# A half pass of the attention scores in two row groups of TensorE: 2.5 passes instead of 3, and 1.5 instead of 2

## The chip, the cores and the metric

One core of one Trainium2 chip. The time is the device time of one execution in microseconds. Three runs of the kernel before gave 3068.02 us (median), 3061.11 and 3082.16.

## The reference, cut to what matters

One layer of a hybrid diffusion transformer on 2048 latent and 256 context tokens, all of it in float32. Two kinds of attention read the same modulated input; the queries are the 2048 latent tokens, the keys all 2304.

```python
q_mla = jnp.concatenate([q_nope, q_rope], axis=-1)     # 8 heads, 64 + 32 features
k_mla = jnp.concatenate([k_nope, broadcast(k_r)], axis=-1)   # the 32 rotary features are shared by the heads
s = jnp.einsum('bhqd,bhkd->bhqk', q, k) * scale        # the scores; softmax over all keys; then p @ v
...
s1 = jnp.einsum('bhqd,bhkd->bhqk', q1, k1) * scale     # 4 heads, two maps of 64 features each
s2 = jnp.einsum('bhqd,bhkd->bhqk', q2, k2) * scale
p = softmax(s1) - lam * softmax(s2)                    # then p @ v
```

After that come gates, an output projection for each kind, a merge, a last projection and a layer norm.

## The kernel before

**Precision.** Float32 operands are split into a high part, rounded to the array's 32-bit form, and a low part, the rest. A product is the sum of high x high, high x low and low x high. Queries and keys are stored in scratch memory with both parts (`qn_s`, `qr_s`, `kn_s`, `kr_s` for the first kind, `dq_s`, `dk_s` for the second; the last index but one is the feature, an axis of 2 the part).

**Stages.** First the projections (0 to 930 us in the profile): weights are loaded, split and multiplied with the transposed inputs in blocks of 512 tokens; `up` and `tiles_qk` write queries and keys to scratch through `rdma`, on SyncE's queue. Then the attention (930 to about 2640 us), then the gated output projections and the last one.

**The attention.** A unit is 256 queries of one head. The units of the two kinds take turns, two of the first (`mla_soft`) and one of the second (`diff_soft`), 64 and 32 in all; the values' products of a unit (`mla_av` at L723 and L728, `diff_av` at L710) run four units later, in pieces between the pieces of the scores, and the projections of the remaining gates (`gate_units`, tiles `pf`) fill in. The order on each engine is set when the program is made, by priorities and a model of the machine. `softmax_tile` makes the scores of 128 queries against all 2304 keys, in three groups of 768 keys. A group has a PSUM tile of two banks (1024 places, 768 used: 512 in the first bank, 256 in the second), of which there are three in turn; the products are at L669. VectorE reads the group at L670 with one instruction that scales and keeps the running extreme; ScalarE takes the exponential of all 2304 (L683). `transposed` makes two 16-bit parts (ScalarE L693, GpSimd L694) and has DMA transposes on SyncE's queue (L695) write them to the `pt` tiles that the values' products read.

**The passes.** The first kind has 96 features, in 96 of the array's 128 rows, and three passes: high x high, high x low, low x high, so 3 x 2 products a group. The second kind keeps the two parts of its keys one above the other, 64 + 64 rows, and its queries twice: one pass with the queries' high part gives high x high and high x low, a second with the queries' low part gives low x high and low x low, so 2 x 2 products. Each product loads its weights, 128 queries, anew. The narrow value products at L728 use 64 of the array's columns, two key tiles at a time in the two halves of the columns.

**Loads.** `load_k` and `load_q` fetch keys once a head and queries once a unit through `ldma` (L604), on ScalarE's queue from the fourth unit on. For the first kind that is two loads a group of keys and two a unit of queries; for the second kind one load a group of keys and two a unit of queries.

Of the kernel before, what the change touches and what calls it, by code (L numbers as in the profile page):

```python
# [61 lines left out]
def layer_kernel(ctx: ExitStack, tc: tile.TileContext, x, c, ctxt, c_ctx, w_mod, b_mod, w_in,  # L62
# [21 lines left out]
    kn_s = [dram(f"kn{t}", [P, 2, NT], F32) for t in range(4)]  # L84
    kr_s = dram("kr", [32, 2, NT], F32)
# [30 lines left out]
    def rsqrt(tp, ms, n):  # L116
        """1/sqrt(ms) of [P, n], one Newton step after the table's root"""
# [10 lines left out]
    def row_rsqrt(tp, ps, s2, cnt, eps):  # L128
        """1/sqrt(sum of squares over the partitions / cnt + eps), on all partitions: [P, 256]"""
# [24 lines left out]
    # the sums of the exponentials: by token, of the heads of both kinds  # L154
# [4 lines left out]
    with ExitStack() as st:  # L159
# [41 lines left out]
        # lamc: -lam, 1 + NT |lam|, shift of the first map  # L201
# [4 lines left out]
        # the log of about 2^15 / (1 + NT |lam|), from the bits of the float  # L206
# [69 lines left out]
        def weights(c0, m):  # L276
# [3 lines left out]
            for j0 in range(0, KT, nj):  # L280
# [3 lines left out]
                # the narrow tile's parts lie side by side, for one pass  # L284
# [20 lines left out]
        def project(w, bi, m, sub):  # L305
            """one tile's product with a block, features by tokens; of a wide tile, 256 tokens by features"""
# [29 lines left out]
        def paired(tiles, blocks):  # L336
            """the tiles (column, width, what to do with a block's product) in pairs, block by block"""
# [24 lines left out]
        def tiles_qk(blocks):  # L362
# [4 lines left out]
            def done(t):  # L367
                m = P if t >= 0 else 32

                def f(bi, pp, n, k0, i0):  # L370
# [14 lines left out]
                    if t < 0:  # L385
                        rdma(kr_s[:, :, k0:k0 + n], s[:m, :, :n])
                        return
# [83 lines left out]
        def up(ui, cn):  # L471
# [12 lines left out]
            for tt in range(2):  # L484
                pb = two(wkv, 2, cn[0], tt * 256)
                s = sq.tile([P, 2, 2, 256], F32R, tag="st", name="kst")
                split(pb, s[:, 0], s[:, 1])
                for a in range(2):
                    rdma(kn_s[2 * tt + a][:, :, k0:k0 + 256], s[:, :, a, :])
# [76 lines left out]
        # for the gates that are left for the attention's idle cycles  # L566
# [11 lines left out]
    with ExitStack() as st:  # L578
# [21 lines left out]
        # the first loads must not hold up the scalar engine, which still works on the projections  # L600
# [60 lines left out]
        def softmax_tile(qk, ks, scale, shift, zsum):  # L661
            s = spool.tile([P, NT], F32, tag="s", name="s")
            z = sm.tile([P, 4], F32, tag="z", name="z")
            for g in range(3):
                ps = ps_s.tile([P, 1024], F32, tag="ps", name="ps")
                for i, (qa, sel) in enumerate(qk):
                    ka = sel(ks[g])
                    for c0, n in ((0, 512), (512, 256)):
                        pe.matmul(ps[:, c0:c0 + n], qa, ka[:, c0:c0 + n], start=(i == 0), stop=(i == len(qk) - 1))  # L669
                dve.tensor_scalar(s[:, g * 768:(g + 1) * 768], ps[:, :768], -scale, 3e38 if g == 0 else z[:, g - 1:g],  # L670
                                  op0=ALU.mult, op1=ALU.min, accum_out=z[:, g:g + 1])
            # the exponent's shift must not push the largest one over: it vanishes, or falls, as |max| grows
# [43 lines left out]
        def mla_av(pts, vv, dst):  # L716
            """both parts of the values by the probabilities' high part; the values' high part by the low part,
            two key tiles at once in halves of the array's columns"""
# [18 lines left out]
        def load_q(kind, h, u):  # L737
            q0 = u * 256
            if kind == 0:
                qt = qp_[0].tile([P, 2, 256], F32R, tag="q0", name="q0")  # L740
                ldma(qt[0:64], qn_s[h // 2][(h % 2) * 64:(h % 2) * 64 + 64, :, q0:q0 + 256])
                ldma(qt[64:96], qr_s[h // 4][(h % 4) * 32:(h % 4) * 32 + 32, :, q0:q0 + 256])
# [6 lines left out]
        def mla_soft(h, u, qt, ks, pts):  # L749
            for i in range(2):  # L750
                qs = qt[0:96, :, i * P:(i + 1) * P]
                k_hi, k_lo = (lambda k: k[0:96, 0, :]), (lambda k: k[0:96, 1, :])
# [308 lines left out]
```

## Time and profile before

| what | us |
|---|---|
| median of 3 runs | 3068.02 (3061.11 to 3082.16) |
| the profiled execution, its span from first to last instruction | 3066.9 |
| projections, 0 to 930 | 930 |
| attention, 930 to 2640 | 1710 |
| output, 2640 to 3067 | 427 |

The page gives no other time for the profiled execution than its span. Busy times of engines overlap each other; a busy time of TensorE (PE) counts each product until its modelled end, so that products which follow closely overlap, and the distance from start to start is what one costs. PEld is the loading of the weights, which runs under the product before it.

### The profile page before, as it was taken

What the parts mean: (1) busy time and instruction counts of PE and PEld (TensorE: products, weight loads), DVE (VectorE), ACT (ScalarE), POOL (GpSimd) and SP (SyncE); (2) the same over time, 40 slices, a digit from 0 to 9 for tenths busy, and PEclk for the clock granted to TensorE, in tenths of its full rate; (3) what the DMA queues carried; (4) which work ended last, traced back from release to release, by engine and by line L of the source; (5) the groups of instructions that cost most, each with busy time, mean ns of one, the idle gap of its engine ahead of it and who ended that gap; (6) DMA issues with size and microseconds to landing.
All of it is one profiled execution on the core that took longest, in us unless ns stands there. A gap on an engine that the chain in (4) does not pass through costs nothing. (4 is left out here: it accounts for less than half of the span.)

```text
span 3066.9 us, 44697 instructions
## 1 busy us (share of the span) xinstructions
PE 2754.2 (90%) x16177; PEld 2233.1 (73%) x16177; DVE 1972.1 (64%) x3583; ACT 1446.4 (47%) x1757; POOL 1558.5 (51%) x922
## 2 busy tenths in 40 slices
PE   7999999999998988978987889989788987888998
PEld 5888888879776766756665676767566765888986
DVE  4476300024857877859887688787687889675454
ACT  3333222233325656647666567666566666321110
POOL 2442222232534756646665567576466655464344
PEclk9999999999999989989999999999899988999999
DMA  8567533264587999999999999999999999976542
GB/s 252 134 181 226 155 92 98 89 222 141 150 256 171 198 178 204 198 187 211 194 206 202 218 219 216 194 216 189 189 213 201 201 207 178 257 208 198 185 139 85
DMA packets 1273377, 571.93 MB, mean 186 GB/s; under 512 B 950250, under 2 KB 1222336, under 8 KB 1273156
## 3 DMA queue, kind: packets, MB, share of 16 engines
q1 hardware_dynamic: 1149448, 463.59, 70.2%
q10 hardware_dynamic: 123708, 105.49, 15.0%
q8 instruction: 127, 2.08, 0.3%
q14 instruction: 94, 0.77, 0.1%
HBM read 224.16 MB, written 118.30 MB: 112 GB/s over the span
## 5 line engine op out<-in xcount | busy, mean ns | idle before, releaser
L694 POOL TENSOR_TENSOR hl<-s,hl 128x1152 f16<-128x1152 f32 x378 | 937.7, 2497 | 542.1 <-ACT hl L693 479.7
L669 PE MATMUL ps<-k,q 96*128 96x256 f32 (+3 forms) x3840 | 858.0, 364 | 110.0 <-DVE s L670 101.5
L669 PEld LDWEIGHTS ps<-k,q 96*128 96x128 f32 (+1 forms) x3840 | 632.3, 200 | 243.8 <-DVE s L670 134.9
L683 ACT ACTIVATE s<-s,z 128x2304 f32<-128x2304 f32 x256 | 567.1, 2216 | 145.7 <-DVE z L681 65.6
L693 ACT CAST hl<-s 128x1152 f16<-128x1152 f32 x384 | 432.3, 1147 | 397.9 <-DMA pt<-hl 226.6
L670 DVE TENSOR_SCALAR_CACHE_REDUCE s<-ps,z 128x768 f32<-128x768 f32 x512 | 517.7, 1013 | 156.6 <-PE ps L669 142.1
L112 PE MATMUL pp<-hT,w 128*128 128x512 f32 (+1 forms) x896 | 349.2, 392 | 5.5 <-DVE qa L331 2.8
L113 PE MATMUL pp<-hT,w 128*128 128x512 f32 (+1 forms) x896 | 350.9, 392 | 0.2 <-DVE hT L266 0.2
L114 PE MATMUL pp<-hT,w 128*128 128x512 f32 (+1 forms) x896 | 349.7, 391 | 0.0
L108 POOL TENSOR_TENSOR w<-raw,w 128x512 fp32r<-128x512 f32 (+1 forms) x126 | 163.5, 1303 | 358.5 <-ACT w L105 343.7
L670 DVE TENSOR_SCALAR_CACHE_REDUCE s<-ps 128x768 f32<-128x768 f32 x256 | 243.4, 951 | 51.4 <-PE ps L669 40.3
L710 PE MATMUL po<-pt,vd 128*128 128x256 f16 x1728 | 241.4, 284 | 31.4 <-DMA pt<-hl 31.1
L723 PE MATMUL po<-pt,va 128*128 128x256 f16 x1152 | 175.5, 294 | 68.3 <-DMA pt<-hl 62.8
L710 PEld LDWEIGHTS <-vd 128*128 128x128 f16 x1728 | 158.6, 102 | 91.3 <-issue 55.6
L112 PEld LDWEIGHTS pp<-hT,w 128*128 128x128 f32 x896 | 169.8, 190 | 44.7 <-DVE qa L331 3.2
L773 DVE SCALAR_TENSOR_TENSOR s<-s,w 128x2304 f32<-128x2304 f32 x64 | 199.3, 3114 | 0.5
L113 PEld LDWEIGHTS pp<-hT,w 128*128 128x128 f32 x896 | 169.7, 189 | 38.5 <-POOL hT L266 0.9
L114 PEld LDWEIGHTS pp<-hT,w 128*128 128x128 f32 x896 | 169.9, 190 | 37.9
L723 PEld LDWEIGHTS <-va 128*128 128x128 f16 x1152 | 106.4, 104 | 120.4 <-issue 79.3
L995 PE MATMUL pz<-wz,yt 128*128 128x512 f32 x768 | 179.6, 396 | 0.8 <-DVE z L998 0.8
L108 POOL TENSOR_TENSOR fw<-fraw,fw 128x512 fp32r<-128x512 f32 x84 | 124.2, 1479 | 90.9 <-ACT fw L105 79.9
L995 PEld LDWEIGHTS pz<-wz,yt 128*128 128x128 f32 x768 | 144.3, 188 | 35.8 <-DVE z L998 1.3
(222 smaller groups left out, 4511.5 us busy)
## 6 DMA issues: line engine op xcount, KB each, us to landing
raw<-in_w_in_dram SPq DMA_DIRECT2D x122, 256.0 KB, 3.1
fraw<-in_w_in_dram ACTq DMA_DIRECT2D x79, 256.0 KB, 4.6
xt<-in_x_dram SPq DMA_DIRECT2D x32, 512.0 KB, 4.7
mg<-gt SPq DMA_DIRECT2D x64, 256.0 KB, 4.2
q<-dq ACTq DMA_DIRECT2D x60, 256.0 KB, 5.6
gt<-o SPq DMA_DIRECT2D x54, 256.0 KB, 2.0
gt<-fo ACTq DMA_DIRECT2D x42, 256.0 KB, 4.8
kn<-kst SPq DMA_DIRECT2D x36, 256.0 KB, 3.3
```

The costliest lines, as they stand in the source:

```text
L108: eng_lo.tensor_tensor(lo, t32, hi.bitcast(F32) if hi.dtype == F32R else hi, op=ALU.subtract)
L112: pe.matmul(ps, wh, mh, start=first, stop=False)
L113: pe.matmul(ps, wh, ml, start=False, stop=False)
L114: pe.matmul(ps, wl, mh, start=False, stop=last)
L669: pe.matmul(ps[:, c0:c0 + n], qa, ka[:, c0:c0 + n], start=(i == 0), stop=(i == len(qk) - 1))
L670: dve.tensor_scalar(s[:, g * 768:(g + 1) * 768], ps[:, :768], -scale, 3e38 if g == 0 else z[:, g - 1:g], op0=ALU.mult, op1=ALU.min, accum_ ...
L683: mark[0] = act.activation(s, s, AF.Exp, bias=b, scale=-1.0, accum_out=zsum).ins
L693: act.copy(hl[:, 0], se)
L694: (dve if shared and e else pool).tensor_tensor(hl[:, 1], se, hl[:, 0], op=ALU.subtract)
L710: pe.matmul(po, vv[:, w, kt, :], pt_part(pts, kt, l), start=(kt == 0 and i == 0), stop=(kt == NKT - 1 and i == 2))
L723: pe.matmul(po, vv[:, kt, :], pt_part(pts, kt, 0), start=(kt == 0), stop=(kt == NKT - 1))
L995: pe.matmul(pz[:, n, :], y[:, yy, k, :], wz[k][ww][:, n * 512:(n + 1) * 512], start=(k == 0 and i == 0), stop=(k == KT - 1 and i == 2))
```

## The change

The third pass of the first kind (and the second of the second kind) is cut into what is needed and packed. For the first kind, whole pass 0 has 128 rows: the query's high part of the 64 plain features against the keys' high and low parts of them. Whole pass 1 has again 128 rows: the plain low part against the keys' high part (64 rows), and twice the 32 rotary features' high part of the query, against the high and the low part of the rotary keys. The rest is 32 rows: the rotary low part against the rotary keys' high part. For the second kind the first pass stays, and the second takes the queries' low part against the keys' high part alone, 64 rows. This rest is run for the two PSUM banks in different rows of the array: bank 0 in rows 64 to 95 and bank 1 in rows 96 to 127 for the first kind, rows 0 to 63 and 64 to 127 for the second. For that the second bank's keys lie with their parts swapped, so that the part that is wanted lies in those rows. Every group now has 384 keys in each bank, and six or four products of 384 columns as before in number. VectorE reads the two 384s by a two-level pattern. `kn_s` is kept by head and part, `kr_s` by part. The loads grow: four of queries a unit of the first kind, five a group of its keys, three a group of the second kind's keys; the store of the plain keys is cut in two. Doc strings and comments that the change drops are left out here.

```diff
-    kn_s = [dram(f"kn{t}", [P, 2, NT], F32) for t in range(4)]
-    kr_s = dram("kr", [32, 2, NT], F32)
+    kn_s = [dram(f"kn{h}", [2, 64, NT], F32) for h in range(H)]
+    kr_s = dram("kr", [2, 32, NT], F32)
...
-                        rdma(kr_s[:, :, k0:k0 + n], s[:m, :, :n])
+                        rdma(kr_s[:, :, k0:k0 + n].rearrange("l d n -> d l n"), s[:m, :, :n])
...
                 for a in range(2):
-                    rdma(kn_s[2 * tt + a][:, :, k0:k0 + 256], s[:, :, a, :])
+                    for e in range(2):
+                        rdma(kn_s[4 * tt + 2 * a + e][:, :, k0:k0 + 256].rearrange("l d n -> d l n"),
+                             s[e * 64:(e + 1) * 64, :, a, :])
...
-                for i, (qa, sel) in enumerate(qk):
-                    ka = sel(ks[g])
-                    for c0, n in ((0, 512), (512, 256)):
-                        pe.matmul(ps[:, c0:c0 + n], qa, ka[:, c0:c0 + n], start=(i == 0), stop=(i == len(qk) - 1))
-                dve.tensor_scalar(s[:, g * 768:(g + 1) * 768], ps[:, :768], -scale, 3e38 if g == 0 else z[:, g - 1:g],
+                for i, part in enumerate(qk):
+                    for b in range(2):
+                        qa, ka = part(ks[g], g, b)
+                        pe.matmul(ps[:, b * 512:b * 512 + 384], qa, ka, start=(i == 0), stop=(i == len(qk) - 1))
+                dve.tensor_scalar(s[:, g * 768:(g + 1) * 768].rearrange("p (b n) -> p b n", b=2),
+                                  ps.rearrange("p (b n) -> p b n", b=2)[:, :, :384], -scale, 3e38 if g == 0 else z[:, g - 1:g],
                                   op0=ALU.mult, op1=ALU.min, accum_out=z[:, g:g + 1])
...
-                qt = qp_[0].tile([P, 2, 256], F32R, tag="q0", name="q0")
-                ldma(qt[0:64], qn_s[h // 2][(h % 2) * 64:(h % 2) * 64 + 64, :, q0:q0 + 256])
-                ldma(qt[64:96], qr_s[h // 4][(h % 4) * 32:(h % 4) * 32 + 32, :, q0:q0 + 256])
+                qt = qp_[0].tile([P, 3, 256], F32R, tag="q0", name="q0")
+                qn = qn_s[h // 2][(h % 2) * 64:(h % 2) * 64 + 64, :, q0:q0 + 256]
+                qr = qr_s[h // 4][(h % 4) * 32:(h % 4) * 32 + 32, :, q0:q0 + 256]
+                ldma(qt[0:64, 0:2], qn)
+                ldma(qt[64:128, 0], qn[:, 0])
+                ldma(qt[64:96, 1:3], qr)
+                ldma(qt[96:128, 1:3], qr)
...
+                qs = qt[:, :, i * P:(i + 1) * P]
+
+                def whole(l):
+                    return lambda k, g, b: (qs[:, l], k[:, l, b * 384:(b + 1) * 384])
+
+                def rest(k, g, b):
+
+                    r = slice(64 + b * 32, 96 + b * 32)
+                    return qs[r, 2], k[r, 1, b * 384:(b + 1) * 384]
+
+                s = softmax_tile([whole(0), whole(1), rest], ks, MLA_SCALE, LN_PSC,
...
+                    def high(k, g, b):
+                        return qs[:, 0, :], k[:, m, b * 384:(b + 1) * 384]
+
+                    def low(k, g, b):
+
+                        r = slice(b * 64, (b + 1) * 64)
+                        return qs[r, 1, :], k[r, m, b * 384:(b + 1) * 384]
+
+                    return softmax_tile([high, low], ks, DIFF_SCALE, shift, zsum)
...
-                    ldma(k[0:64], kn_s[h // 2][(h % 2) * 64:(h % 2) * 64 + 64, :, cs])
-                    ldma(k[64:96], kr_s[:, :, cs])
+                    ldma(k[:, 0, :], kn_s[h][:, :, cs].rearrange("l d n -> (l d) n"))
+                    ldma(k[0:64, 1, :], kn_s[h][0, :, cs])
+                    ldma(k[64:128, 1, 0:384], kr_s[:, :, g * 768:g * 768 + 384].rearrange("l d n -> (l d) n"))
+                    for l in range(2):
+                        ldma(k[96 - l * 32:128 - l * 32, 1, 384:768], kr_s[l, :, g * 768 + 384:(g + 1) * 768])
                 else:
-                    ldma(k, dk_s[h][:, :, :, cs].rearrange("l d m n -> (l d) m n"))
+                    cs = slice(g * 768, g * 768 + 384)
+                    ldma(k[:, :, 0:384], dk_s[h][:, :, :, cs].rearrange("l d m n -> (l d) m n"))
+                    cs = slice(g * 768 + 384, (g + 1) * 768)
+                    for l in range(2):
+                        ldma(k[(1 - l) * 64:(2 - l) * 64, :, 384:768], dk_s[h][l, :, :, cs])
```

## Rows read from the trace of the kernel before

**Rows 1.** The page's first part: busy us of each engine, share of the span, instructions.
```profile
PE 2754.2 (90%) x16177; PEld 2233.1 (73%) x16177; DVE 1972.1 (64%) x3583; ACT 1446.4 (47%) x1757; POOL 1558.5 (51%) x922
```

**Rows 2.** Busy time by stretch: us, each engine's busy us, clock, DMA share, GB/s.
```profile
core 0: us, PE busy (x) PEld busy (x) DVE busy (x) ACT busy (x) POOL busy (x), PEclk, DMA share, GB/s
0.00:930.00 930.00, 884.66 (x4738) 735.63 (x4739) 365.89 (x676) 275.43 (x523) 294.94 (x254) 0.99 0.56 168
930.00:2640.00 1710.00, 1481.99 (x8996) 1151.65 (x8996) 1371.35 (x2402) 1099.83 (x1094) 1069.36 (x476) 0.92 1.09 199
```

**Rows 3.** Chain of waits, 1836 to 2640 us: shares of the stretch by line.
```profile
by line: DMA pt<-hl 19.3%; issue 14.8%; PE ps L669 11.0%; DVE s L670 10.5%; POOL hl L694 6.4%; ACT s L683 4.0%; ACT hl L693 3.4%; PE po L710 3.2%; DVE s L773 2.7%; PE po L723 2.4%; DMA fraw<-in_w_in_dram 2.1%; PE po L728 1.6%; SPq L695 1.4%
```

**Rows 4.** Groups by line: scores' products and PSUM reads; count, busy us, mean ns.
```profile
L669 PE MATMUL ps<-k,q 96*128 96x256 f32 (+3 forms) x3840 | 858.0, 364 | 110.0 <-DVE s L670 101.5 <-ACT o L417 5.0 <-issue 2.7
L670 DVE TENSOR_SCALAR_CACHE_REDUCE s<-ps,z 128x768 f32<-128x768 f32 x512 | 517.7, 1013 | 156.6 <-PE ps L669 142.1
L670 DVE TENSOR_SCALAR_CACHE_REDUCE s<-ps 128x768 f32<-128x768 f32 x256 | 243.4, 951 | 51.4 <-PE ps L669 40.3 <-POOL hl L694 9.7
```

**Rows 5.** Timeline of TensorE, 1502.7 to 1508.9: start us, us, what, how many.
```profile
1502.79 1.30 PE L669 MATMUL ps<-k,q 96*128 96x512 f32 x6
1503.93 0.39 PE L710 MATMUL po<-pt,vd 128*128 128x256 f16 x2
...
1506.73 1.05 PE L710 MATMUL po<-pt,vd 128*128 128x256 f16 x8
1507.53 0.94 PE L669 MATMUL ps<-k,q 128*128 128x512 f32 x4
1508.32 0.72 PE L710 MATMUL po<-pt,vd 128*128 128x256 f16 x5
```

**Rows 6.** Timeline of TensorE around narrow f16 products, 1521.0 to 1524.2.
```profile
1521.03 0.49 PE L723 MATMUL po<-pt,va 128*128 128x256 f16 x3
1521.45 0.30 PE L728 MATMUL po<-pt,va 128*64 128x256 f16 x1
1521.67 0.96 PE L669 MATMUL ps<-k,q 128*128 128x512 f32 x4
1522.57 0.73 PE L728 MATMUL po<-pt,va 128*64 128x256 f16 x9
1523.23 0.96 PE L669 MATMUL ps<-k,q 128*128 128x512 f32 x4
1524.12 0.30 PE L728 MATMUL po<-pt,va 128*64 128x256 f16 x2
```

**Rows 7.** Waits of the weight loads, 930 to 2640: us in total, times, longest.
```profile
PEld L723 <- issue: 79.1, 174, 14.8
PEld L728 <- issue: 46.4, 159, 2.7
```

**Rows 8.** Timeline of TensorE at 870.8: products on one row, then on one column.
```profile
870.80 0.38 PE L526 MATMUL pvb<-vrow,ones 1*128 1x2 f32 x2 [2.76 <-DVE vrow L524]
871.11 0.27 PE L520 MATMUL pvm<-ident,vm 128*1 128x128 f32 x1
```

**Rows 9.** Timeline of TensorE at 114.5: f32 products of 64 and 32 columns by turns.
```profile
114.54 2.04 PE L316 MATMUL pp<-hT,w 128*64 128x256 f32 x16
116.42 0.28 PE L112 MATMUL pp<-hT,w 128*128 128x256 f32 x1
```

**Rows 10.** Issues of loads and stores: ns of one, min/median/max, first and last start.
```profile
L604 ACTq DMA_DIRECT2D q<-qn x62: 519/529/1259, 955.8 to 2553.7; - x62
L604 ACTq DMA_DIRECT2D q<-qr x62: 573/650/1818, 959.5 to 2555.4; - x62
...
L143 SPq DMA_DIRECT2D kn<-kst x36: 518/615/1311, 148.1 to 847.5; - x36
```

More of the change, by code (lines that the diff above doesn't have):

```diff
@@ L750, in mla_soft @@
             for i in range(2):
-                qs = qt[0:96, :, i * P:(i + 1) * P]
-                k_hi, k_lo = (lambda k: k[0:96, 0, :]), (lambda k: k[0:96, 1, :])
-                s = softmax_tile([(qs[:, 0, :], k_hi), (qs[:, 0, :], k_lo), (qs[:, 1, :], k_hi)], ks, MLA_SCALE, LN_PSC,
+                qs = qt[:, :, i * P:(i + 1) * P]
[5 more added lines that the diff above has]
+                s = softmax_tile([whole(0), whole(1), rest], ks, MLA_SCALE, LN_PSC,
                                  zs[u][:, i, h:h + 1])
@@ L761, in scores @@
                     qs = qt[:, m, :, i * P:(i + 1) * P]
-                    km = (lambda k: k[:, m, :])
-                    return softmax_tile([(qs[:, 0, :], km), (qs[:, 1, :], km)], ks, DIFF_SCALE, shift, zsum)
+                    def high(k, g, b):
[4 more added lines that the diff above has]
+                    return softmax_tile([high, low], ks, DIFF_SCALE, shift, zsum)
                 za = zs[u][:, i, H + h:H + h + 1]
```

## The prediction

> **What bounds the kernel now.** I read the page's head first, then the window table by stage, then the chain of waits in the attention, and last the single products of TensorE. The page's head shows TensorE busy 90% of the span and VectorE 64% [rows 1]. The window table puts the stage that the change touches at 930 to 2640 us: 1710 us, in which TensorE is busy 1482, VectorE 1371, ScalarE 1100, and the DMA share is 1.09 at 199 GB/s; before it, in the projections, TensorE is busy 885 of 930 us and DMA only 0.56 [rows 2]. So in the attention no engine is the bound by itself. The chain of waits says the same: over 1836 to 2640 us the transposes' landings hold 19.3%, "issue" 14.8%, the scores' products 11.0%, the PSUM reads 10.5%, and the three kinds of value products 7.2% together [rows 3]. A microsecond saved or added on TensorE lands in part only. The scores' products are busy 858 us of the 1710, and the 768 groups of PSUM reads (512 + 256) tell how many times a group of 768 keys is made [rows 4].
>
> **Step 1, columns saved.** A group of the first kind streams 3 x 768 columns, of the second 2 x 768. In a run of products without a break, six take 1502.79 to 1503.93, 1.14 us, and four 1507.53 to 1508.32, 0.79 [rows 5]. The first is recorded early: the eight f16 products before the four are 0.11 us apart ((1.05 - 0.72)/(8 - 5)), so the last of them starts at 1507.50, and 0.08 of it is still streaming. That leaves 1.06 and 0.71 us, so 768 columns cost 0.35 and 384 cost 0.175. Both kinds now stream 384 fewer columns a group if the two halves of the last pass run side by side: -0.175 us each, 768 times, -134 us. Equal products of 384 columns instead of 512 and 256 change nothing else: the weight load lies under the product before it in both shapes.
>
> **Step 2, what it costs to enter and leave the half pass.** The trace has no product that shares the array's rows, so I bound it by the nearest, the f16 products on 64 columns at L728. The last of three full products starts at 1521.25 (1521.03 and twice 0.11), the first narrow one only at 1521.45: 0.20 us instead of 0.11, so 0.09 is lost on the way in. One narrow product alone holds the array from 1521.45 to 1521.67, 0.22 instead of 0.11, and nine (five slots of 0.11, as they run in pairs) 1522.57 to 1523.23, 0.66 instead of 0.55: 0.11 for its own short load and the way out. A scores' group of four between two such batches takes 0.90 and 0.89 us (1521.67 to 1522.57, 1523.23 to 1524.12) instead of 0.71: the way out again, 0.09, and 0.105 because its first f32 load no longer hides under another product [rows 6]. The loads' queue has this idle time under "issue": 79.1 us in 174 pieces and 46.4 in 159 [rows 7]. The Trainium skill (TensorEngine Tiling (Array Packing), Key Properties) says that changing the tiling mode, not just the tile, drains the engine; the trace agrees with 0.09 us a change; by the rule the half pass is drained like these, by [rows 9] it isn't, which is +119 against -134 us below. Whether the array's rows behave like its columns is open: the only product on few rows is followed after two tiny products by 0.31 us (870.80 to 871.11) without a wait [rows 8], while sixteen narrow f32 products, 64 and 32 columns by turns, run 114.54 to 116.42, 0.118 apart, with no loss at all [rows 9]. I take the price of [rows 6], since there too two parts of the array work at once, as the change wants.
>
> Per group: 0.09 in, 0.105 for the load of the halves (both at once), 0.175 streaming, 0.09 out, and 0.02 (f16) to 0.105 (f32) for the next product's load, in place of 0.35: +0.13 to +0.215 for both kinds. Where narrow products follow, the way out was paid already. I take +0.155: 768 x 0.155 = +119 us of TensorE time. The ends: -134 us if nothing is drained and the loads hide; if the halves don't overlap (+0.175) and their loads follow one another (+0.105), 768 x (0.215 + 0.28) = +380 us.
>
> **How much of it lands.** TensorE has 228 us idle in the stage, and the scores' 11.0% of the chain against 50% busy (858/1710) means that 22% of their time is on it: 26 us. At the other end all 119 land. Part of the chain's "issue" is the drain itself, and the slower engine moves onto the chain, so I take half: +59 us. What is late next is the PSUM read at L670, and behind it the exponential and the transposes.
>
> **Step 3, more to load.** A unit of the first kind loads 320 KB of queries instead of 192, 64 times, and a group of keys 768 KB instead of 576, 24 times: 8.4 + 4.7 = 13.1 MB, at 199 GB/s 66 us if DMA were the only bound. The transposes and loads hold about 21% of the chain: +14 us; ends 0 and +66.
>
> **Step 4, more issues on ScalarE's queue.** Queries go from two issues to four (+128), keys from two to five (+72) and from one to three (+24): 224 at 0.53 to 0.65 us [rows 10], 132 us in ScalarE's order, ahead of exponentials and casts. ScalarE is busy 1100 of 1710, and issues run under a running activation; its work holds 7.4% of the chain (4.0 + 3.4), so +10, and I take +13 with the waits that an issue adds; ends 0 and +66 (half exposed). On SyncE's queue 36 more stores of keys at 0.615 us [rows 10], 22 us in 930, lie under the projections' products: 0, and 22 if that cover were gone. The PSUM read takes the same 768 elements over the same two banks: 0; ends -5 and +20 for its other cut.
>
> **Sum.** 59 + 14 + 13 = +86 us on the profiled execution's 3066.9 us span: 3153, and 1 us more for the median of 3068.02, which stands 1.1 above that span: **3154 us**.
>
> **Rivals.** *Row halves don't drain (faster).* For it: [rows 9], f32 products of changing width without loss. Against: [rows 6]. TensorE then saves up to 134 us, of which 22% to 60% land, -30 to -80, and steps 3 and 4 give 0 to 27 back: 2990 to 3060, middle 3025. It decides where the four losses of a group together stay under 0.175 us. The Trainium skill (TensorEngine Tiling, Theoretical Speedup) promises up to 2x for a contraction of 64 or less and 4x for 32, and by that table alone this would be the result. *The slack takes it up.* For it: 228 us idle, and a chain with TensorE on a quarter of it. Then 26 + 0 to 27: 3065 to 3098. *The halves don't run side by side.* Then the change doesn't do what it says: 119 + 134 = 253 us, 60% landing, plus 27: about 3247; for it speaks only that no row shows such a pair. *The clock falls.* The granted clock is 0.92 in the stage and 0.99 in the projections, where the engine is denser [rows 2]: 0.92 is 16% of the time at 1.2 GHz, the rest at 2.4. A drained engine streams less; were it 0.86, 28% at 1.2, then 12% of 1710 us, 205, run at half rate, and with half of the lost 100 us landing the time is 3204.
>
> **How the numbers follow.** The forecast has 0.58 (its own range 3107 to 3225), the drain-free rival 0.14, the slack 0.15, the serial halves 0.07, the clock 0.06. A measurement tells about 1% from no change, 3037 to 3099. Faster by over 1%: most of the drain-free case, 0.11. Within 1%: the slack, the rest of the drain-free case and a little of the forecast, 0.20. Slower: 0.69. The range leaves out the lower part of the drain-free case and the upper part of the serial halves: 3040 to 3245.
>
> **What would show it.** Step 1: the half pass as two products whose starts lie some ns apart. Step 2: 0.28 us or more from the last full product to the half pass, and the load queue's idle time under "issue" ahead of L669's successor grown by over 100 us. Step 3: a higher DMA share per us and longer landings of the transposes. If successive products at the change of shape lie 0.175 us apart, step 2 is wrong and the drain-free rival holds; if they are drained and the time still stays within 1%, my landing share is wrong.

## The result, and the profile after

The changed kernel takes 3111.39 us (median of four, 3105.49 to 3127.16), the kernel before 3071.46 beside it (four, 3061.11 to 3082.16): the ratio is 1.0127 [1.0097, 1.0157], 39 us slower. The profiled execution of after has a span of 3110.6 us against 3066.9. So the forecast's direction came true and its size did not: +39 us instead of +86.

The page's head, busy us of each engine (before in [rows 1]):

```profile
PE 2846.5 (92%) x16177; PEld 2146.6 (69%) x16177; DVE 1966.0 (63%) x3583; ACT 1450.9 (47%) x1757; POOL 1568.5 (50%) x922
```

TensorE has the same 16177 products, of fewer columns, and is busy 92.3 us **longer** (2846.5 against 2754.2). The span grew by 43.7. The rest, 48.6 us, came out of TensorE's idle time: 3066.9 - 2754.2 = 312.7 us before, 3110.6 - 2846.5 = 264.1 after. So the change made TensorE's work longer, and at least half of that vanished in waits that TensorE had anyway. The 43.7 us hold what the loads cost as well; the experiments below part the two.

Busy time by stretch, as in [rows 2]:

```profile
0.00:930.00 930.00, 888.05 (x4739) 739.64 (x4739) 364.06 (x676) 276.49 (x523) 296.98 (x254) 0.99 0.57 166
930.00:2640.00 1710.00, 1542.78 (x8801) 1037.67 (x8801) 1338.38 (x2357) 1083.04 (x1064) 1061.42 (x463) 0.93 1.12 203
```

In the attention TensorE is busy 61 us more (1482 before) while it gets through 195 fewer of its products (8801 of 8996): the attention's last value product starts at 2668 us instead of 2645. The granted clock stayed (0.92 before, 0.93), the DMA share went from 1.09 to 1.12. Chain of waits, 1836 to 2640 us (cut at its end by the view; before in [rows 3]):

```profile
by line: DMA pt<-hl 21.9%; issue 14.6%; PE ps L671 13.9%; POOL hl L697 7.3%; DVE s L672 5.2%; ACT hl L696 4.0%; PE po L713 3.4%; PE po L726 3.3%; ACT s L686 2.9%; ACTq L606 2.3%; DMA k<-kr 2.1%; PE po L731 1.9%; PE pf L114 1.5%; POOL fw L10
```

The scores' products (now L671) hold 13.9% instead of 11.0, the PSUM reads (L672) 5.2 instead of 10.5: TensorE moved onto the chain where VectorE had been.

One group of the first kind, first TensorE's products, then the loads of their weights (start us, us, what, count):

```profile
1500.04 0.60 PE L726 MATMUL po<-pt,va 128*128 128x256 f16 x4
1500.40 1.32 PE L671 MATMUL ps<-k,q 128*128 128x384 f32 x6
1501.65 0.50 PE L726 MATMUL po<-pt,va 128*128 128x256 f16 x3
```

```profile
1500.37 0.66 PEld L671 LDWEIGHTS ps<-k,q 128*128 128x128 f32 x4
1501.27 0.18 PEld L671 LDWEIGHTS ps<-k,q 32*128 32x128 f32 x2 [0.25 <-issue]
1501.64 0.22 PEld L726 LDWEIGHTS <-va 128*128 128x128 f16 x3 [0.19 <-issue]
```

The single records behind these lines show the whole price (a product that has to wait for its weight load is recorded from that load on). The four full products start at 1500.399, .659, .836 and 1501.006. The half products start at 1501.275 and 1501.278, 3 ns apart, and their two loads, of 181 ns each, lie as close: so they take 0.18 us for both, not 0.36, and the two row groups do run side by side. But their load begins 0.267 us after the last full product, its 0.175 us of streaming and 0.09 more; and the next f16 load begins 0.37 us after theirs: with the prediction's 0.105 for their own load and 0.175 of streaming, 0.09 are left for the way out. From the last full product to that next load are 0.638 us, where two more full products would have taken 0.35 and the last one's own 0.175. The group takes 1.25 us from start to start against 1.14 in [rows 5]. This group is the rule: over all 768 the median is 0.268 us from the last full product to the half pass.

The Trainium skill (TensorEngine Tiling (Array Packing), Key Properties) says that a change of the tiling mode drains the engine; the 0.09 us before the half pass and the 0.09 after it agree. The Trainium skill (TensorE: Matmul & The Clock Gate, Part 3) has tiles of different rows start about 4 ns apart; here it is 3.

Waits in the attention, 930 to 2640 us (us in total, times, longest):

```profile
PEld ps L671 <- issue: 240.5, 931, 4.1
PE ps L671 <- DVE s L672: 69.2, 52, 4.7
PE po L726 <- DMA pt<-hl: 39.3, 10, 9.4
PE po L713 <- DMA pt<-hl: 20.9, 11, 4.6
PE po L731 <- DMA pt<-hl: 6.2, 6, 2.4
```

The first is new, 240.5 us in 931 pieces: it is the drain as the load queue sees it, once per group and more (16.2 us in 60 pieces before). The others are waits from which it is paid: TensorE waited 101.5 us for PSUM reads [rows 4] before and 69.2 now.

### The profile page after: what moved, and what is told of

It is laid out like the page before. It is cut to its first block, busy times and chain, and to the rows that moved or that the text cites. A ratio compares the mean times of both kernels' runs of the same rounds, so it can differ in the third digit from the quotient of the medians.

```text
span 3110.6 us, 45115 instructions
## 1 busy us (share of the span) xinstructions
PE 2846.5 (92%) x16177; PEld 2146.6 (69%) x16177; DVE 1966.0 (63%) x3583; ACT 1450.9 (47%) x1757; POOL 1568.5 (50%) x922
## 4 chain that ended last, share of the span: by engine, by line
PE 47%; DMA 22%; DVE 9%; issue 8%; POOL 5%; ACT 5%; SPq 2%; ACTq 1%; POOLq 0%; DVEq 0%
DMA pt<-hl 13%; PE ps L671 8%; PE pp L112 7%; PE pp L113 7%; PE pp L114 7%; PE pz L1026 6%; POOL hl L697 3%; DVE s L672 3%; PE po L713 2%; ACT hl L696 2%; ACT s L686 2%; PE po L726 2%; DMA fraw<-in_w_in_dram 1%; DMA mg<-gt 1%; PE po L731 1%
## 5 line engine op out<-in xcount | busy, mean ns | idle before, releaser
L671 PE MATMUL ps<-k,q 128*128 128x384 f32 (+2 forms) x3840 | 888.7, 403 | 72.5 <-DVE s L672 69.2
L671 PEld LDWEIGHTS ps<-k,q 128*128 128x128 f32 (+2 forms) x3840 | 539.7, 192 | 364.0 <-issue 240.5
L672 DVE TENSOR_SCALAR_CACHE_REDUCE s<-ps,z 128x768 f32<-128x768 f32 x512 | 518.5, 1014 | 148.6 <-PE ps L671 134.1
L672 DVE TENSOR_SCALAR_CACHE_REDUCE s<-ps 128x768 f32<-128x768 f32 x256 | 243.8, 952 | 76.2 <-PE ps L671 61.1
L713 PE MATMUL po<-pt,vd 128*128 128x256 f16 x1728 | 241.2, 284 | 22.8 <-DMA pt<-hl 22.3
L713 PEld LDWEIGHTS <-vd 128*128 128x128 f16 x1728 | 157.1, 101 | 83.3 <-issue 57.7
L108 POOL TENSOR_TENSOR fw<-fraw,fw 128x512 fp32r<-128x512 f32 x84 | 130.8, 1557 | 108.3 <-ACT fw L105 98.3
```

Source lines behind the costliest of these rows:

```text
L108: eng_lo.tensor_tensor(lo, t32, hi.bitcast(F32) if hi.dtype == F32R else hi, op=ALU.subtract)
L671: pe.matmul(ps[:, b * 512:b * 512 + 384], qa, ka, start=(i == 0), stop=(i == len(qk) - 1))
L672: dve.tensor_scalar(s[:, g * 768:(g + 1) * 768].rearrange("p (b n) -> p b n", b=2), ps.rearrange("p (b n) -> p b n", b=2)[:, :, :384], -sc ...
L713: pe.matmul(po, vv[:, w, kt, :], pt_part(pts, kt, l), start=(kt == 0 and i == 0), stop=(kt == NKT - 1 and i == 2))
```

## The experiments

The change has two parts that can be taken separately: the packed half pass, and the loads with the layout that feed it. A third thing comes along unasked: the order of the work is planned from a cost of each operation, so nearly every edit gives another order on the engines. Laid side by side place by place in the traces, TensorE's 16177 products (by the tile that they write and their columns) come in the same order in after, e3 and e4 below, and e1 agrees with after in 99.4% of the places, so these four can be compared like with like. Before and after agree in 66%, s1 and s2 in 81%.

### The half pass: whole, gone, in the same rows, joined

**e1_whole** keeps the layout, the loads and the 384 columns, and runs the last pass as whole products (for the first kind a repeat of its second pass):

```diff
-                s = softmax_tile([whole(0), whole(1), rest], ks, ...
+                s = softmax_tile([whole(0), whole(1), whole(1)], ks, ...
...
-                        return qs[r, 1, :], k[r, m, b * 384:(b + 1) * 384]
+                        return qs[:, 1, :], k[:, m, b * 384:(b + 1) * 384]
```

> The changed kernel's layout, loads and 384-column products, but the half pass runs as a whole 128-row product for each bank (for the first kind it repeats the second pass, so its scores count that pass twice): columns as before the change, no change of the array's shape, all the new loads and issues. Theory A (the drains around the half pass cost more than its columns save; about 100 us more TensorE work, part of which lands): the packing alone is what costs, so without it 3071 to 3085. Rival B (the packing is neutral and the 13 MB and 224 issues more are what costs): 3100 to 3115, as the changed kernel. Rival C (the planner's new order holds back the output products until the last value product): 3090 to 3098, whatever the scores do, if the order stays as in the changed kernel.

**e2_nohalf** leaves the half pass out, and with it the products of the queries' low parts that it holds:

```diff
-                s = softmax_tile([whole(0), whole(1), rest], ks, ...
+                s = softmax_tile([whole(0), whole(1)], ks, ...
...
-                    return softmax_tile([high, low], ks, DIFF_SCALE, shift, zsum)
+                    return softmax_tile([high], ks, DIFF_SCALE, shift, zsum)
```

> The changed kernel without the half pass (2 and 1 whole passes; the products with the queries' low part are left out, for the first kind the rotary ones alone): against the kernel with a whole pass in its place 768 times 0.35 us less TensorE work, 269 us; against the changed kernel about 370 us less. Theory A with a landing share of 0.2 to 0.5: 2950 to 3020. Rival B (loads and issues set the pace): not under 3060.

**e3_same_rows** puts both halves into the same rows, so that they can't overlap (the second bank meets the other part of its keys):

```diff
-                    r = slice(64 + b * 32, 96 + b * 32)
+                    r = slice(64, 96)
...
-                        r = slice(b * 64, (b + 1) * 64)
+                        r = slice(0, 64)
```

> The changed kernel with both banks' half products in the same rows of the array (the second bank then meets the other part of its keys): they can't run side by side, 768 times 0.175 us more TensorE work, 134 us, with the same drains and loads. Theory A, share 0.2 to 0.5: 27 to 67 us over the changed kernel, 3138 to 3178; in the trace the second half starts 0.175 us after the first. Rival B: 3110, no change.

**e4_joined** runs the half pass first in every second group, so that two half passes meet where the groups are neighbours, and two changes of shape in four fall away there:

```diff
+                turn[0] += 1
-                for i, part in enumerate(qk):
+                for i, part in enumerate(qk if turn[0] % 2 else qk[-1:] + qk[:-1]):
```

> The changed kernel with the half pass first in every second group, so that the half passes of two neighbouring groups meet and the array changes shape once for both; it does so only where the order on TensorE has the two groups next to each other, about a quarter of the groups. Theory A: 90 joins at most at 0.2 to 0.3 us each, 18 to 27 us of TensorE work, landing 5 to 13: 3098 to 3106. Rival B: 3111.

Measured: e1 3095.47 us, 1.0064 [1.0036, 1.0092]; e2 3069.85, 0.9943 [0.9905, 0.9981]; e3 3148.77, 1.0225 [1.0169, 1.0281]; e4 3118.25, 1.0123 [1.0077, 1.0170]. Only e3 came out inside its range by theory A. e1 lies above theory A's 3071 to 3085, since without the packing the kernel is still 20 us slower than before; it falls into rival C's range, but C, an order that holds the output back, can't explain steps between kernels whose order is the same. e2 misses theory A's 2950 to 3020 by 50 us and lies where rival B, loads and issues that set the pace, had it; against B stand e1, after and e3, which differ by 19 and 30 us with the same loads. e4 misses its 3098 to 3106 by 12. The page's heads of e1, e3 and e2:

```profile
PE 2749.8 (89%) x16177; PEld 2295.0 (74%) x16177; DVE 1958.5 (63%) x3583; ACT 1449.4 (47%) x1757; POOL 1565.8 (51%) x922
```

```profile
PE 2968.7 (94%) x16177; PEld 2230.7 (71%) x16177; DVE 1963.0 (62%) x3583; ACT 1452.8 (46%) x1757; POOL 1552.6 (49%) x922
```

```profile
PE 2553.3 (83%) x14641; PEld 2069.7 (67%) x14641; DVE 1942.6 (63%) x3583; ACT 1449.7 (47%) x1757; POOL 1576.6 (51%) x922
```

Three kernels with one order (e4 is the fourth, below) make a scale on which only TensorE's work grows:

| step | TensorE busier | span longer | share that lands |
|---|---|---|---|
| e1 to after | 2846.5 - 2749.8 = 96.7 | 3110.6 - 3096.0 = 14.6 | 0.15 |
| after to e3 | 2968.7 - 2846.5 = 122.2 | 3147.4 - 3110.6 = 36.8 | 0.30 |

(By the ratios the steps are 0.0063, 19 us, and 0.0098, 30 us: shares of 0.20 and 0.25.) The half pass as it stands costs TensorE **more** than the whole pass that it replaces, 97 us, and only a sixth of it lands, 15 to 19. That the share rises from the first step to the second is seen in the single executions alone; the two ratio steps are known to 0.004 and 0.006, too wide to tell 0.20 from 0.25. It fits the waits that absorb the work, which are being used up. Here they are for e1 and for e3, to be laid beside those of after above:

```profile
PE ps L671 <- DVE s L672: 103.3, 65, 9.2
PE po L726 <- DMA pt<-hl: 66.1, 15, 10.8
PE po L713 <- DMA pt<-hl: 43.9, 17, 9.3
PE po L731 <- DMA pt<-hl: 9.9, 9, 1.9
```

```profile
PE ps L671 <- DVE s L672: 27.1, 18, 5.4
PE po L726 <- DMA pt<-hl: 19.6, 5, 5.7
PE po L731 <- DMA pt<-hl: 18.6, 4, 7.7
PE po L713 <- DMA pt<-hl: 8.9, 3, 4.5
```

TensorE's waits for PSUM reads go 103.3, 69.2, 27.1; those for the transposes 119.9, 66.4, 47.1. From e1 to after they shrink by 34 + 53 = 87 us, as much as the 82 us by which TensorE's idle time shrank over the whole run (346.2 to 264.1). This is where the expected loss went: a TensorE that is slower comes later to waits that would have held it. The chain says the same. That of e1 can be followed back only to 2144 us, so these are e1, after and e3 from 2144 to 2640 us:

```profile
by line: DMA pt<-hl 28.3%; issue 14.3%; DVE s L672 9.4%; PE ps L671 7.5%; POOL hl L697 6.8%; ACT hl L696 3.4%; DMA vraw<-vd 3.1%; DVE s L797 2.1%; SPq L698 2.1%; PE po L726 1.8%; DVE z L679 1.8%; ACT s L686 1.7%; POOL fw L108 1.7%; PE po L7
```

```profile
by line: DMA pt<-hl 21.0%; PE ps L671 15.4%; issue 14.7%; POOL hl L697 8.6%; DVE s L672 4.0%; PE po L726 4.0%; PE po L713 3.7%; DMA k<-kr 3.4%; ACT hl L696 3.3%; ACT s L686 2.4%; PE po L731 2.2%; ACTq L606 1.9%; PE pf L114 1.8%; DMA k<-dk 1
```

```profile
by line: PE ps L671 33.1%; DMA pt<-hl 13.1%; PE po L713 10.3%; issue 6.6%; PE po L726 5.8%; PE po L731 3.5%; DVE s L672 3.5%; PE pf L114 3.3%; PE pf L112 3.1%; PE pf L113 3.0%; DMA k<-kr 1.8%; POOL hl L697 1.3%; SPq L698 1.3%; DMA oa<-o 1.1
```

The scores' products hold 7.5%, 15.4% and 33.1%, the transposes 28.3%, 21.0% and 13.1%: with e3 TensorE's products together hold over 60% of the chain. That the halves of after overlap is shown by e3 too: its six products take 1.45 us where after's take 1.25.

```profile
1504.94 1.52 PE L671 MATMUL ps<-k,q 128*128 128x384 f32 x6
1506.39 0.30 PE L731 MATMUL po<-pt,va 128*64 128x256 f16 x2
```

e2, with 196.5 us less on TensorE than e1, is 25.5 us of span below it (share 0.13; by the ratios 37 us, 0.19): this layout without any half pass lies only 0.6% under the kernel before, in an order of its own. The products left out were to save 269 us. In e2 the granted clock of the attention is 0.87, against 0.93 in e1, and the same 1728 value products at L713 are busy 253.3 us instead of 238.0: an emptier TensorE ran at the lower clock level for longer, and part of the saving went that way.

e4 keeps after's order; only the half pass's place in its group differs. In 85 places two half passes meet, and the changes between row shapes fall from 1536 to 1366. The first two lines show a group that begins with its half pass, the others two groups whose half passes meet, twelve products in a run:

```profile
1502.60 0.50 PE L728 MATMUL po<-pt,va 128*128 128x256 f16 x3
1503.03 1.34 PE L673 MATMUL ps<-k,q 32*128 32x384 f32 x6
...
1510.46 2.43 PE L673 MATMUL ps<-k,q 128*128 128x384 f32 x12
1512.82 0.62 PE L733 MATMUL po<-pt,va 128*64 128x256 f16 x7
```

Where they meet, the second half pass takes 0.177 us (0.549 from the first to the next full product, where one alone takes 0.372), without a drain and a load of its own. But TensorE is busy 6.8 us more than in after (2853.3). Most of the other 299 groups that begin with their half pass pay it back. A group of the second kind between two runs of full-width f16 products takes 1.034 us with the half pass first and 0.93 with it last (medians of 90 and 110), 0.105 more, about what the prediction gave for an f32 load that no product hides: here that of the first full product, behind the half pass.

### A product of two by two: packing and loads

**s1_384** is the kernel before with two 384s in place of 512 and 256; **s2_pack_only** adds the packed last pass to that and nothing else, with the loads of before (its halves meet a part of the features, and the second bank's another part of the keys). Both against before:

```diff
-                    for c0, n in ((0, 512), (512, 256)):
-                        pe.matmul(ps[:, c0:c0 + n], qa, ka[:, c0:c0 + n], ...
+                    for b in range(2):
+                        r = slice(0, qa.shape[0])
+                        if i == len(qk) - 1:                      # s2 alone
+                            m = 32 if len(qk) == 3 else 64
+                            r = slice(b * m, (b + 1) * m)
+                        pe.matmul(ps[:, b * 512:b * 512 + 384], qa[r], ka[r, b * 384:(b + 1) * 384], ...
```

> The kernel before with 384 and 384 keys in the two banks instead of 512 and 256, nothing else: same columns, loads and issues. Prediction: 0, 3069 to 3080. If the run with whole passes lay 26 us under the one with the loads alone because of the shape, this one would be near 3050.

> That kernel with the last pass packed, but with the loads and the keys' places of before: the halves take rows 0 to 31 and 32 to 63 (first kind) or 0 to 63 and 64 to 127 (second), so they meet only part of the features, or the other part of the keys in the second bank. TensorE's work as in the changed kernel, about 100 us more by my sum, without its loads and issues. Theory A' (the drains land with a share of 0.15 to 0.3): 3088 to 3105. Theory B (the packing is neutral, loads and issues are all): 3070 to 3080. Prediction as written, half landing: 3125.

Measured: s1 3077.36, 1.0009 [0.9982, 1.0035]; s2 3095.35, 1.0061 [1.0026, 1.0096]. With e1 and after this fills a table of ratios:

| | loads and layout of before | loads and layout of after |
|---|---|---|
| whole last pass | s1 1.0009 | e1 1.0064 |
| packed last pass | s2 1.0061 | after 1.0127 |

Packing costs 0.0052 with the one layout and 0.0063 with the other, 16 and 19 us; loads and layout cost 0.0055 and 0.0066, 17 and 20 us. That the parts add up to the 39 us is arithmetic; what the table shows is that each is about half, and that neither changes the other's price beyond the noise (each difference is known to about 0.004). Only the step from e1 to after has one order. s1 and s2 differ in theirs, and in the granted clock of the attention (0.93 and 0.91), and TensorE is busy 141.7 us more in s2 (2879.9 against 2738.2) where the like step adds 97; between the layouts, too, the order differs. The cut into equal products is worth nothing, as the prediction had it.

### What in the loads costs the 17 to 20 us: not settled

Six kernels are the kernel before with other loads of the same or of unused data. **p2_loads** makes all of after's extra loads, unused; **p3_issues** cuts loads so that there are 224 more issues for the same bytes; **s3_bytes** loads 384 queries instead of 256 in each load of the first kind (6.3 MB, no issue more); **w3_more_issues** has 480 more issues, **w4_more_bytes** 10.5 MB more; **p1_place** only makes the query tile as large as after's. The forms of the edits, from p3 and s3:

```diff
-                ldma(qt[0:64], qn_s[h // 2][(h % 2) * 64:(h % 2) * 64 + 64, :, q0:q0 + 256])
+                for a in range(2):
+                    ldma(qt[a * 32:(a + 1) * 32], qn_s[h // 2][(h % 2) * 64 + a * 32:(h % 2) * 64 + a * 32 + 32, :, q0:q0 + 256])
...
-                qt = qp_[0].tile([P, 2, 256], F32R, tag="q0", name="q0")
+                qt = qp_[0].tile([P, 2, 384], F32R, tag="q0", name="q0")
+                q1 = min(q0, NL - 384)
+                ldma(qt[0:64], qn_s[h // 2][(h % 2) * 64:(h % 2) * 64 + 64, :, q1:q1 + 384])
```

> The kernel before with all the changed kernel's extra loads and issues (13.1 MB, 224 issues) into parts of the tiles that nothing reads; the larger query tile makes the same late order as in the run with the tile alone. Theory D: the loads add at most 10 us to the larger tile's time, 3090 to 3105. Theory B: 3095 to 3105 while the larger tile alone is at 3076.

> The kernel before with its loads cut so that there are 224 issues more for the same bytes; the order on TensorE is the one of before. If the issues in ScalarE's order cost what the prediction gave them, 13 us and up to 66: 3085 to 3140. Theory D: 3073 to 3081.

> The kernel before with query loads of the first kind half as long again (384 tokens, of which 256 are used): 6.3 MB more, no issue more, about half of the changed kernel's 13.1 MB. If bytes cost what the difference of the loads' run and the issues' run says (22 us for 13.1 MB): 3084. If only issues cost: 3074. The prediction's share of the chain (14 us for 13.1 MB): 3080.

> The kernel before with 480 issues more for the same bytes (the run with 224 more cost 18 us). If the cost goes with the number: 38 us, 3108 to 3118. If that run only fell on a worse order: 3080 to 3095.

> The kernel before with longer query loads for both kinds: 10.5 MB more, no issue more (the run with 6.3 MB more cost 30 us). If the cost goes with the bytes: 50 us, 3115 to 3130. If it is at most the transfer's own time at 199 GB/s times a share of the chain: 3085 to 3095.

> The kernel before with one change: the tile of the first kind's queries is a third larger and its third part is never used (2 KB more in each partition over the two buffers). Same work, loads and products. In the planned order on TensorE the 72 value products that stood behind the first output product now all stand ahead of it, as in the changed kernel. Theory D (about half of the changed kernel's loss is this shift in the place of tiles, which holds the output stage back until the last value product): 3090 to 3100, with the attention's end where it was and the output products starting 40 us later. Theory B (loads and issues cost the 20 us between the kernel before and the one with whole passes): 3076, no change.

Two more move a pool (`cvr`) to the other side of the memory, in after (**p4_packed_place**) and in before (**w1_place_before**), because in after every value product of the last units ran ahead of the output's first product, while in before 72 of them came behind it:

```diff
-        vr = st.enter_context(tc.tile_pool(name="cvr", bufs=2))
...
+        vr = st.enter_context(tc.tile_pool(name="cvr", bufs=2, side="right"))
```

> The changed kernel with the two buffers of raw values moved to the other side of the memory, so that 36 of the 72 value products stand behind the first output product again; nothing else differs. Theory D: half of the 20 us comes back, 3098 to 3104. If the place has no part in it: 3111.

> The kernel before with the two buffers of raw values moved to the other side of the memory, as in the run of the changed kernel that this made 16 us faster. If the place itself is worth that: 3055 to 3062, faster than both kernels. If it only undid something of the changed kernel: 3070 to 3078.

| kernel | us | ratio |
|---|---|---|
| p1, larger tile alone | 3075.30 | 0.9988 [0.9959, 1.0016] |
| p2, +13 MB and 224 issues | 3121.41 | 1.0129 [1.0090, 1.0167] |
| p3, +224 issues | 3093.29 | 1.0059 [1.0031, 1.0086] |
| w3, +480 issues | 3104.16 | 1.0086 [1.0053, 1.0119] |
| s3, +6.3 MB | 3112.26 | 1.0097 [1.0067, 1.0127] |
| w4, +10.5 MB | 3112.24 | 1.0104 [1.0062, 1.0146] |
| p4, after with the pool moved | 3095.30 | 1.0060 [1.0033, 1.0087] |
| w1, before with the pool moved | 3082.97 | 1.0021 [0.9999, 1.0043] |

Of what was expected, p1 came out as theory B had it and p3 inside its range; p2 and s3 are slower than any of their theories, w3 and w4 fall between theirs, p4 is faster than its range and w1 slower than both of its. More loading is slower in each of them, but not in proportion: twice the issues are not twice the cost (18 and 26 us), and two thirds more bytes cost the same (30 and 32 us). p2, with all the loads and none of the packing, costs 40 us, and e1, with the same loads in use, 20. Each has its own order, so an effect of 20 us or so that comes with the order can't be parted from the loads. p1 and w1 refute that the place of the tiles is the cause (nothing, and +6 us with an interval that reaches 1); p1 agrees with before in 96% of TensorE's places and has all 72 value products ahead of the output, as after has; p4 gained 16 us on after all the same, with another order, for which I have no cause that a run shows.

**s4_more_pe** was to give the share that plain TensorE work has when it is added to before: the last product of 256 columns in each group is made once more (so the scores of those keys hold that part twice).

```diff
+                pe.matmul(ps[:, 512:768], qa, ka[:, 512:768], start=False, stop=True)
```

> The kernel before with the last product of 256 columns of every group made twice (its term counts twice): 768 times 0.117 us, 90 us more TensorE work without a drain, a load or an issue. It gives the landing share of TensorE's time from above: 0.15 to 0.3 by theory A', 3087 to 3100; half by the prediction, 3118; none if the drains and not the engine's time are what counts, 3074.

It measured 3119.18, 1.0125 [1.0092, 1.0159]; TensorE 93.6 us busier (2847.8), the span 37.5 longer, a share of 0.40: the 3118 that the prediction's half had given. But the planner prices the extra product and spreads the gates' products out to 2641.7 us instead of 2450: not like with like, and no bound for after's share.

### A version that is faster than both

**w2_fewer_issues** goes the other way: the queries of the first kind are kept by head, plain and rotary features one above the other, so that a unit needs one load instead of two (64 issues fewer, 80 more stores in the projections).

```diff
-    qn_s = [dram(f"qn{t}", [P, 2, NL], F32) for t in range(4)]
-    qr_s = [dram(f"qr{t}", [P, 2, NL], F32) for t in range(2)]
+    q_s = [dram(f"q{h}", [96, 2, NL], F32) for h in range(H)]
...
-                ldma(qt[0:64], qn_s[h // 2][(h % 2) * 64:(h % 2) * 64 + 64, :, q0:q0 + 256])
-                ldma(qt[64:96], qr_s[h // 4][(h % 4) * 32:(h % 4) * 32 + 32, :, q0:q0 + 256])
+                ldma(qt[0:96], q_s[h][:, :, q0:q0 + 256])
```

> The kernel before with the first kind's queries kept by head with both their parts in one place, so that a unit loads them with one issue instead of two: 64 issues fewer on ScalarE's queue, 80 stores more on SyncE's in the projections, same bytes. By the run with 224 issues more (18 us): 5 us less, 3065 to 3072. If issues cost nothing: 3075.

**x1_packed_3issues** does the like for after (three loads a unit instead of four), **x2_one_issue** adds to w2 that the second kind's queries are stored twice and loaded with one issue.

> The changed kernel with the first kind's queries kept by head, the rotary part twice, so that a unit loads them with three issues instead of four: 64 issues fewer on ScalarE's queue, same bytes, more stores on SyncE's queue in the projections. Taking one issue a unit away from the kernel before gave 18 us. If an issue ahead of each unit's scores has that price wherever it stands: 3093. If the gain needs a single issue: 3108 to 3114.

> The kernel before with one query issue a unit for both kinds (the second kind's doubled queries are stored twice): 96 issues fewer than before, 32 fewer than the run that was 18 us faster. By that price, 0.28 us an issue: 3048 to 3054; if the second kind's have no part: 3059. Either way faster than both kernels.

w2 measured 3059.49, 0.9941 [0.9912, 0.9970]: faster than both kernels, by 0.6% and 1.8%, and faster than the 3065 to 3072 expected. x1 measured 3113.05, 1.0134 [1.0096, 1.0171], no gain on after, and x2 3101.79, 1.0087 [1.0060, 1.0114], 1.5% **slower** than w2 though it issues less still: a miss. So that fewer issues make w2 fast is not shown; its order may do it.

## Why the prediction was wrong in size

**The bound** was read rightly: no engine by itself, TensorE on a part of the chain. **Step 1** holds: two half products 3 ns apart, 0.175 us for both; e3, without the overlap, costs 30 to 37 us more.

**Step 2** holds in every term: 0.09 in, 0.105 for the load, 0.175, 0.09 out, and the price of [rows 6] carries over from columns to rows of the array. The sum was +119 us; measured are +97 (e1 to after) or +92 (before to after), 0.12 to 0.13 us a group instead of 0.155. What follows the group decides, as the range +0.13 to +0.215 had it (medians in e1 and after): 0.115 more where full-width f16 products follow (0.815 to 0.93 us for a group of the second kind between two runs of them), 0.11 on top where f32 products follow, for their first load, and almost nothing among narrow products (1.47 to 1.483 us for a group of the first kind), which pay the change of shape anyway. The signature that was named is there: 0.269 us from the last full product to the half pass, where 0.28 was asked, and 240 us of "issue" at the load queue.

**"How much of it lands" is the step that failed.** The text set 22% as the lower end, from the chain's 11.0% against 50% busy, and then took half because the slower engine moves onto the chain; no row stood behind the half. The engine does move (7.5% in e1, 15.4% in after), but by a step of 97 us it had only begun to: 15 to 19 us landed, 0.15 to 0.20, against the 59 predicted. The plain reading of the chain, 0.22 x 97 = 21 us, would have hit. Read from each kernel's own chain, the rule gives for e1 7.5% against 51% busy (251 of 496 us), 0.15 x 97 = 14 us, and for after 15.4% against 53% (264 of 496), 0.29 x 122 = 35 us; the spans grew by 14.6 and 36.8. The waits that can absorb TensorE's work were there to be read before: its 101.5 us for PSUM reads [rows 4], and for the transposes, 930 to 2640 us in before:

```profile
PE po L723 <- DMA pt<-hl: 59.7, 14, 14.3
PE po L710 <- DMA pt<-hl: 31.1, 15, 5.8
PE po L728 <- DMA pt<-hl: 11.3, 11, 2.4
```

Together 203.6 us, twice what the step adds; after still has 135.6 of them (69.2 + 39.3 + 20.9 + 6.2).

**Step 4**'s issues took what [rows 10] said, a median of 0.55 and 0.61 us for the queries' two loads. **Steps 3 and 4** gave 14 + 13 = 27 us; the loads and layout measured 17 to 20 together. In sum that is near, but it may be luck: the split between bytes and issues, and what part is the order, stays open. The expected signs of step 3 are there and small: DMA share 1.12 for 1.09, and the median from issue to landing of the transposes, in before and in after:

```profile
pt<-hl SPq DMA_TRANSPOSE x384, 6.3
```

```profile
pt<-hl SPq DMA_TRANSPOSE x384, 6.7
```

**The sum** with the measured terms, packing 16 to 19 and loads with layout 17 to 20, makes up the 39 us, against 59 + 27. **The rivals:** that row halves don't drain is refuted by the timeline (0.09 us each way, every group), serial halves by their 3 ns, the falling clock by 0.93. The slack rival had the right mechanism and the right first term, 26 us; its upper end should have read 3068 + 26 + 27 = 3121, which would have held the 3111, and not 3098. I gave it 0.15 where the chain's own share spoke for it.

## What to carry to other kernels

A pass split into row groups pays only if what it saves in columns exceeds the way in, the uncovered f32 load and the way out, here 0.175 us saved against about 0.30 lost (0.175 and the 0.12 to 0.13 a group that TensorE became slower); shorten passes that are long, or keep neighbours in one shape (where two half passes meet in e4 the second costs 0.177 us), and see which product's load is laid bare by it. For work added to an engine that is busy 90% but sits on 11% of the chain, take the chain's share (11% / 50%) as the landing share, and raise it only when the waits that would absorb it are smaller than the addition: list those waits and add them up. Two steps at equal order bear this out here; s4, in an order of its own, came out at 0.40. And where an order is planned from costs, compare kernels whose order is equal; moving one pool to the other side of the memory, and the order with it, shifted after by 0.7% (p4).

## What had not been expected of the hardware

Row groups change shape at the same price as column groups: 0.09 us in and 0.09 us out, on 32 rows (first kind) as on 64 (second kind). The loads of the two halves wait for it alike, by form over the whole run (us busy, mean ns, idle before):

```profile
L671 PEld LDWEIGHTS ps<-k,q 64*128 64x128 f32 x768 | 73.6, 188 | 99.4 <-issue 99.4
L671 PEld LDWEIGHTS ps<-k,q 32*128 32x128 f32 x768 | 72.7, 186 | 99.9 <-issue 99.9
```

384 pairs of either form wait 0.26 us a pair. The loads overlap only in different rows: in e3's same rows a pair takes 0.29 us instead of 0.18.

```profile
1505.85 0.29 PEld L671 LDWEIGHTS ps<-k,q 32*128 32x128 f32 x2 [0.26 <-issue]
```
